# Two chunks per transpose, and edge key blocks of attention over 128 queries, in a hybrid attention and RWKV-7 block

## The chip, the cores and the metric

The kernel runs on one core of a Trainium2 chip. A core has five engines with a queue each: PE (TensorE, the matmul array, whose weight loads are listed apart as PEld), DVE (VectorE), ACT (ScalarE), POOL (GpSimd) and SP (SyncE, which here only issues transfers). The metric is the time of one execution on the device in microseconds (us), lower is better. Kernels are compared by the median of their runs.

## The reference

One layer over 2048 tokens of width 1024, in float32. Attention and a recurrence run side by side on the same normalised input, are gated and merged, and a feed-forward part follows.

```python
h = rms_norm(x, pre_mix_g); proj = h @ w_in          # q/k/v, rwkv columns, gates
# attention: 8 heads of 64; a chunk of 64 queries sees its own chunk and the 8 before it
scores = q . k * 64**-0.5 + bias[clipped distance]
y_a = softmax(scores) @ v
# RWKV-7: 8 heads of 64, state 64 x 64 per head, scan over time
state = state * w_t + (state @ a_t) b_t + v_t k_t    # a_t = -kk, b_t = kk * a
y = state @ r_t
y_b = (group_norm(y) * ln_x_w + ln_x_b + bonus) * g
merged = sigmoid(gA) * (y_a @ proj_a) + sigmoid(gB) * (y_b @ proj_b)
x = x + rms_norm(merged @ w_out, post_mix_g)
x = x + rms_norm(relu(rms_norm(x) @ w_up)**2 @ w_down, post_ffn_g)
```

## The kernel before

The tokens are worked in four groups of 512 (g = 0 to 3). For each group come a recurrence phase (phase_rwkv), attention (phase_attention) and the merge; after the four groups the feed-forward part (phase_up, phase_down) runs for all tokens. A large product is done with split operands: a float32 matrix is cut into a high and a low part, and three matmuls of 512 columns (hi by hi, hi by lo, lo by hi) replace one exact product. Those of the input projection are called psd (line 75). Each needs a block of weights, loaded by SP (wraw) and split by ACT (whi) and DVE (wlo).

The order of each engine's queue is not the order of the code: a scheduler sorts the instructions engine by engine, by its own estimates, so that psd matmuls fill the gaps of the recurrence and of attention. Any change to a step can move others.

**Recurrence.** Heads are worked in pairs p (the two heads, par = 0 and 1, on partitions 0 to 63 and 64 to 127), in chunks of 64 tokens (8 chunks, c). rwkv_pre forms the scaled operands: AR holds for each chunk three blocks of 64 columns, of which, before, slots 0 and 1 hold the decayed -kk of head 0 and of head 1 on their own rows and products of the chunk (ps_A, masked) on the other rows, and slot 2 the decayed r. rwkv_inverse inverts a unit triangular matrix per chunk by 31 steps on DVE (T and X), for two pairs of heads at a time, so twice in a group; it ends with two transposes on DVE (X, then XD), and PE's ps_t matmuls need the first. rwkv_trans then transposes A on PE (ps_at), ACT copies it into WA, and ps_w, ps_ug, ps_tq and ps_s build the transition of each chunk. recurrence runs the chunks (ps_st). rwkv_post normalises the outputs (yn), transposes them on PE (ps_yt), and ACT writes them with gain and bias into yf.

**Attention.** att_pair works a pair of heads. A half-head is 256 queries of one head, as two query blocks of 128 (b = 0, 1). A query block sees five key blocks of 128. Scores (ps_s) are reduced and exponentiated (sc), transposed on PE (ps_pt), and split by ACT into PTh and by DVE into PTl, both [128, 6 key blocks, 256 queries]. The product with the values (ps_pv, line 855) runs over six key blocks, PTh and then PTl, all 256 queries wide. Key block 0 belongs to query block 0 alone and key block 5 to query block 1 alone; the other 128 columns of these two hold zeros, set once per group (lines 906 and 907).

Of the kernel before, what the change touches and what calls it, by code (L numbers as in the profile page):

```python
# [17 lines left out]
P = 128  # L18
# [7 lines left out]
C = 64  # L26
NC = G // C
# [22 lines left out]
class Block:  # L50
# [75 lines left out]
    def constants(self, ctx, mixing):  # L126
        tc, nc, a = self.tc, self.nc, self.a
        keep = ctx.enter_context(tc.tile_pool(name="const", bufs=1))
        cp = mixing.enter_context(tc.tile_pool(name="mconst", bufs=1, side="right"))
# [38 lines left out]
        for t in self.st:  # L168
# [5 lines left out]
        rows = [("gate_bias", 16), ("shift_mu", 14), ("w0", 4), ("a0", 4), ("k_k", 4),  # L174
                ("k_a", 4), ("r_k", 4), ("ln_x_w", 4), ("ln_x_b", 4)]
# [5 lines left out]
        with tc.tile_pool(name="setup", bufs=1, side="right") as sp, \  # L181
# [18 lines left out]
            ps = pp.tile([P, nrow], F32, name="ps_rows")  # L200
# [43 lines left out]
        self.rk = view("r_k", 4)  # L244
        self.gw = view("ln_x_w", 4)
        self.gb = view("ln_x_b", 4)
        self.gwo = cp.tile([C, 4], F32, name="gwo")
        self.gbo = cp.tile([C, 4], F32, name="gbo")
        nc.vector.tensor_copy(self.gwo, self.gw[C:P])
        nc.vector.tensor_copy(self.gbo, self.gb[C:P])  # L250


        self.kc = [dp.tile([P, 2, G], F32, name=f"kc{p}") for p in range(NP)]
# [90 lines left out]
    def rwkv_pre(self, g, p, rp, NA, between=lambda: None):  # L344
        nc = self.nc
        pc = slice(p * P, (p + 1) * P)
        col = slice(p, p + 1)
# [5 lines left out]
        ps = self.lora(0, p)  # L353
# [50 lines left out]
            )  # L404
        between()

        AR = rp.tile([P, NC, 3, C], F32, tag="AR", name="AR")
        BK = self.tp.tile([P, NC, 2, C], F32, tag="BK", bufs=1, name="BK")
        k3 = k.rearrange("p (c t) -> p c t", t=C)
        r3 = r.rearrange("p (c t) -> p c t", t=C)  # L410
        for par in range(2):
            rw = slice(par * C, par * C + C)
            nc.vector.scalar_tensor_tensor(
                AR[rw, :, par], k3[rw], self.nkk[rw, col], E[rw, :, 0:C], op0=ALU.mult, op1=ALU.mult
            )
        nc.vector.tensor_tensor(AR[:, :, 2], r3, E[:, :, 1 : C + 1], ALU.mult)
        tk = self.tmp("tk")
        nc.scalar.activation(tk, ta, AF.Identity, scale=self.hka[:, col], bias=self.c1[:, col])
        nc.vector.tensor_tensor(tk, tk, k, ALU.mult)
# [50 lines left out]
        for h in range(2):  # L470
            cs = slice(h * 4, h * 4 + 4)

            both = [self.pa.tile([P, 4, P], F32, tag="a", name="ps_A") for _ in range(2)]
            for j in range(4):
                c = h * 4 + j
                for par, psA in enumerate(both):
                    rw = slice(par * C, par * C + C)
                    nc.tensor.matmul(
                        psA[:, j].rearrange("p (s t) -> p s t", t=C),
                        BK[rw, c].rearrange("p s t -> p (s t)"),  # L480
                        AR[rw, c, par : 3 : 2 - par], start=True, stop=True,
                    )
            for par, psA in enumerate(both):
                ow = slice(C - par * C, P - par * C)
                for lo, w in ((0, C), (32, 32)):
                    hw = slice(par * C + lo, par * C + lo + 32)
                    nc.vector.tensor_tensor(
                        NA[hw, q, cs, 0:w],
                        psA[hw, :, lo : lo + w],
                        n2[hw, cs, par, None].to_broadcast((32, 4, w)),  # L490
                        ALU.mult,
                    )
                nc.vector.tensor_tensor(AR[ow, cs, par], psA[ow, :, 0:C], mS[ow], ALU.mult)
                nc.vector.tensor_tensor(BR[:, cs, par, 1], psA[:, :, C:P], mN[:, par, cs], ALU.mult)
        R["AR"], R["BR"] = AR, BR
        return R
# [57 lines left out]
    def rwkv_trans(self, p, R):  # L554

        nc, xp = self.nc, self.xp
        AR, SV, XT, BR = (R[x] for x in ("AR", "SV", "XT", "BR"))
        rows = [slice(0, C), slice(C, P)]
        halves = [slice(0, 4), slice(4, 8)]

        WA = xp.tile([P, NC, 2, C], F32, tag="WA", bufs=1, name="WA")
        for h, cs in enumerate(halves):
            ps = self.pa.tile([P, 4, P], F32, tag="a", name="ps_at")
            for j in range(4):
                nc.tensor.transpose(ps[:, j], AR[:, h * 4 + j, 0:2].rearrange("p s t -> p (s t)"), self.ident)
            for par in range(2):
                nc.scalar.copy(WA[rows[par], cs, 0], ps[rows[par], :, par * C : par * C + C])
        ps = self.pa.tile([P, NC, C], F32, tag="a", name="ps_w")
        for c in range(NC):
            for par in range(2):  # L570
                ow = rows[1 - par]
                nc.tensor.matmul(ps[rows[par], c], AR[ow, c, par], SV[ow, c, par], start=True, stop=True)
        nc.scalar.copy(WA[:, :, 1], ps)
        yield

        GT = xp.tile([P, NC, C], F32, tag="GT", bufs=1, name="GT")
        for h, cs in enumerate(halves):
            ps = self.pa.tile([P, 4, 2, C], F32, tag="a", name="ps_ug")
            for j in range(4):
                c = h * 4 + j  # L580
                for par in range(2):
                    nc.tensor.matmul(ps[rows[par], j], XT[rows[par], c], WA[rows[par], c], start=True, stop=True)
            nc.scalar.copy(GT[:, cs], ps[:, :, 0])
            for par in range(2):
                nc.scalar.copy(SV[rows[par], cs, par], ps[rows[par], :, 1])
        yield
        TQ = xp.tile([P, NC, 2, C], F32, tag="TQ", name="TQ")
        for h, cs in enumerate(halves):
            ps = self.pa.tile([P, 4, 2, C], F32, tag="a", name="ps_tq")
            for j in range(4):  # L590
                c = h * 4 + j
                for par in range(2):
                    nc.tensor.matmul(
                        ps[rows[par], j], GT[rows[par], c], BR[rows[par], c, par], start=True, stop=True
                    )
            nc.vector.tensor_tensor(
                TQ[:, cs, 0], ps[:, :, 0], self.id64[:, None, :].to_broadcast((P, 4, C)), ALU.add
            )
            nc.vector.tensor_tensor(TQ[:, cs, 1], ps[:, :, 1], AR[:, cs, 2], ALU.add)
        yield  # L600
        S0 = xp.tile([P, NC, C], F32, tag="S0", name="S0")
        ps = self.pa.tile([P, NC, C], F32, tag="a", name="ps_s0")
        Y = R["Y"] = self.py.tile([P, NC, C], F32, tag="y", name="ps_y")
        for c in range(NC):
            for par in range(2):
                nc.tensor.matmul(ps[rows[par], c], BR[:, c, par, 0], SV[:, c, par], start=True, stop=True)
        nc.vector.tensor_tensor(S0, ps, R["gC"][:, :, None].to_broadcast((P, NC, C)), ALU.mult)
        for c in range(NC):
            for par in range(2):
                nc.tensor.matmul(Y[rows[par], c], BR[:, c, par, 1], SV[:, c, par], start=c == 0, stop=False)  # L610
        R["TQ"], R["S0"] = TQ, S0
        R["ST"] = xp.tile([P, NC - 1, C], F32, tag="ST", name="ST")
# [16 lines left out]
    def rwkv_post(self, p, R):  # L629
# [13 lines left out]
        yield  # L643
        yf = self.tmp("yf")
        yf3 = yf.rearrange("p (c t) -> p c t", t=C)
        for h in range(2):
            ps = self.pr.tile([C, 4, P], F32, tag="wus", name="ps_yt")
            for j in range(4):
                nc.tensor.transpose(ps[:, j], yn[:, h * 4 + j], self.ident)
            cs = slice(h * 4, h * 4 + 4)  # L650
            nc.scalar.activation(
                yf3[0:C, cs], ps[:, :, 0:C], AF.Identity, scale=self.gw[0:C, col], bias=self.gb[0:C, col]
            )
            nc.scalar.activation(
                yf3[C:P, cs], ps[:, :, C:P], AF.Identity, scale=self.gwo[:, col], bias=self.gbo[:, col]
            )
# [104 lines left out]
    def att_pair(self, g, p):  # L761
# [44 lines left out]
        for par in range(2):  # L806
            bias = self.load_bias(2 * p + par)
            Kv = KK[:, par].rearrange("p h n -> p (h n)")
            for half in range(2):
# [38 lines left out]
                    nc.vector.tensor_tensor(lv, pst[:, 0:nk], hv.bitcast(F32), ALU.subtract)  # L848
                pv = self.pv.tile([P, 2 * P], F32, tag="pv", name="ps_pv")
                kts = [kt for kt in range(6) if not first or half * 2 + kt >= GT]  # L850
                terms = [(x, kt) for x in (PTh, PTl) for kt in kts]
                for i, (x, kt) in enumerate(terms):
                    kb = half * 2 + kt
                    st = VV[:, kb // GT, kb % GT, par].rearrange("p s d -> p (s d)")
                    nc.tensor.matmul(pv, st, x[:, kt], start=i == 0, stop=i == len(terms) - 1)
# [33 lines left out]
    def phase_attention(self, g):  # L889
# [5 lines left out]
        with ExitStack() as ctx:  # L895
# [6 lines left out]
            self.pts, self.npt = [], 0  # L902
            for i in range(2):
                t = [pp.tile([P, 6, 2 * P], F32R, name=f"PT{x}{i}") for x in "hl"]
                for y in t:
                    nc.gpsimd.memset(y[:, 0, P : 2 * P].bitcast(F32), 0.0)
                    nc.gpsimd.memset(y[:, 5, 0:P].bitcast(F32), 0.0)
                self.pts.append(t)
            for p in range(NP):
                self.att_pair(g, p)  # L910
# [389 lines left out]
```

## Time and profile before

| what | value |
|---|---|
| median of 3 runs | 3430.61 us (3426.16 to 3436.8) |
| profiled execution | 3436.05 us, span 3434.4 us |
| granted PE clock, mean | 0.988 |
| PE busy | 3297.5 us (96%), 19233 matmuls |
| DVE busy | 2412.8 us (70%) |
| ACT busy | 1414.1 us (41%) |
| POOL busy | 419.6 us (12%) |
| products of attention (ps_pv) | from 339.3 to 2000.2 us, in four groups |

The span runs from the first instruction to the last. Busy time of PE counts matmuls that overlap in the array once, and the end of a matmul is modelled. A wait is written "engine tile line <- engine tile line": who waited, and whose end released it, with the sum in us, the count and the longest. Line numbers are those of the kernel before.

### The profile page before, as it was taken

What the parts mean: (1) busy time and instruction counts of PE and PEld (TensorE: products, weight loads), DVE (VectorE), ACT (ScalarE), POOL (GpSimd) and SP (SyncE); (2) the same over time, 40 slices, a digit from 0 to 9 for tenths busy, and PEclk for the clock granted to TensorE, in tenths of its full rate; (3) what the DMA queues carried; (4) which work ended last, traced back from release to release, by engine and by line L of the source; (5) the groups of instructions that cost most, each with busy time, mean ns of one, the idle gap of its engine ahead of it and who ended that gap; (6) DMA issues with size and microseconds to landing.
All of it is one profiled execution on the core that took longest, in us unless ns stands there. A gap on an engine that the chain in (4) does not pass through costs nothing. (4 is left out here: it accounts for less than half of the span.)

```text
span 3434.4 us, 50373 instructions
## 1 busy us (share of the span) xinstructions
PE 3297.5 (96%) x19233; PEld 2674.4 (78%) x19233; DVE 2412.8 (70%) x4110; ACT 1414.1 (41%) x2319; POOL 419.6 (12%) x796
## 2 busy tenths in 40 slices
PE   7999999999989999989999989999999999999998
PEld 5777777777867777867777877888888878888886
DVE  5774856766865766865775865877887788676667
ACT  4434634436644435644445634333321243331112
POOL 2210002101022111012210000111200021100001
PEclk9999999999999999999999999999999999999999
DMA  5224353225373125373224276434845374343333
GB/s 146 84 82 130 130 191 113 63 90 191 113 270 123 59 87 181 120 264 123 72 88 143 90 267 217 132 117 148 297 152 182 95 241 135 117 144 98 98 98 110
DMA packets 397864, 481.10 MB, mean 140 GB/s; under 512 B 17516, under 2 KB 304432, under 8 KB 397624
## 3 DMA queue, kind: packets, MB, share of 16 engines
q1 hardware_dynamic: 346168, 364.63, 34.1%
q0 software_dynamic: 23040, 79.71, 6.1%
q10 hardware_dynamic: 28416, 33.56, 2.9%
q8 instruction: 151, 2.47, 0.3%
q14 instruction: 89, 0.73, 0.1%
HBM read 356.16 MB, written 124.81 MB: 140 GB/s over the span
## 5 line engine op out<-in xcount | busy, mean ns | idle before, releaser
L75 PE MATMUL ps_dn<-fop 128*128 128x512 f32 x3072 | 702.6, 390 | 4.1 <-DVE u L1178 4.1
L75 PEld LDWEIGHTS ps_dn<-fop 128*128 128x128 f32 x3072 | 576.7, 188 | 126.2 <-DVE u L1178 6.0
L75 PE MATMUL psd<-hh,whi 128*128 128x512 f32 x1344 | 542.8, 404 | 8.0 <-ACT whi L66 7.1
L75 PE MATMUL psd<-hl,whi 128*128 128x512 f32 x1344 | 541.7, 403 | 0.0
L75 PE MATMUL psd<-hh,wlo 128*128 128x512 f32 x1344 | 538.4, 401 | 0.6 <-DVE wlo L67 0.5
L66 ACT CAST whi<-wraw 128x1024 fp32r<-128x1024 f32 x232 | 243.2, 1049 | 516.9 <-PE psd L75 405.8
L1178 DVE TENSOR_TENSOR u<-u,ps_dn 128x512 f32<-128x512 f32 x480 | 323.3, 685 | 149.5 <-PE ps_dn L75 148.7
L67 DVE TENSOR_TENSOR wlo<-wraw,whi 128x1024 fp32r<-128x1024 f32 x232 | 282.9, 1220 | 199.1 <-ACT whi L66 180.9
L75 PEld LDWEIGHTS psd<-hh,whi 128*128 128x128 f32 x1344 | 256.9, 191 | 60.9 <-ACT whi L66 7.9
L75 PEld LDWEIGHTS psd<-hh,wlo 128*128 128x128 f32 x1344 | 256.5, 191 | 50.5 <-DVE wlo L67 2.0
L75 PEld LDWEIGHTS psd<-hl,whi 128*128 128x128 f32 x1344 | 256.8, 191 | 50.0
L66 ACT CAST fop<-wdraw 128x1024 fp32r<-128x1024 f32 x64 | 67.0, 1047 | 427.4 <-PE ps_dn L75 236.0
L1099 POOL DMA_DIRECT2D ad<-r x128 | 69.2, 541 | 586.3 <-DVE r L1098 570.2
L968 PE MATMUL ps_o<-whi,mh 128*128 128x512 f32 x256 | 103.4, 411 | 16.6 <-ACT whi L66 12.3
L75 PE MATMUL ps_p<-yh,whi 128*128 128x512 f32 x256 | 103.8, 405 | 14.6 <-DVE th L939 12.7
L66 ACT CAST s12h<-s 128x1024 fp32r<-128x1024 f32 x32 | 33.7, 1054 | 184.6 <-PE ps_u L75 184.6
L831 DVE CUSTOM_DVE_ANT_0 sc<-bias,ps_s 128x640 f32<-128x640 f32 (+4 forms) x128 | 93.4, 730 | 22.3 <-PE ps_pt L843 18.1
L836 ACT ACTIVATE sc<-sc,mn 128x640 f32<-128x640 f32 (+4 forms) x128 | 97.7, 764 | 19.3 <-DVE mn L831 18.5
L75 PE MATMUL ps_p<-yh,wlo 128*128 128x512 f32 x256 | 104.2, 408 | 0.1
L847 ACT CAST PTh<-ps_pt 128x640 fp32r<-128x640 f32 (+4 forms) x128 | 80.0, 625 | 58.7 <-PE ps_pt L843 57.6
L75 PE MATMUL ps_p<-yl,whi 128*128 128x512 f32 x256 | 103.5, 404 | 0.0
L1097 ACT ACTIVATE r<-r 128x512 f32<-128x512 f32 x128 | 80.7, 630 | 54.2 <-DVE r L1096 54.0
(352 smaller groups left out, 6668.2 us busy)
## 6 DMA issues: line engine op xcount, KB each, us to landing
wraw<-in_w_in_dram SPq DMA_DIRECT2D x168, 512.0 KB
wraw<-in_w_up_dram SPq DMA_DIRECT2D x80, 512.0 KB
ad<-r POOLq DMA_DIRECT2D x128, 256.0 KB, 2.4
wdraw<-in_w_down_dram SPq DMA_DIRECT2D x64, 512.0 KB
araw<-ad SPq DMA_DIRECT2D x64, 512.0 KB
gd<-gate ACTq DMA_DIRECT2D x64, 256.0 KB
th<-gd SPq DMA_DIRECT2D x32, 512.0 KB
wraw<-in_w_out_dram SPq DMA_DIRECT2D x32, 512.0 KB
```

Source lines behind the costliest of these rows:

```text
L66: self.nc.scalar.copy(hi, src)
L67: self.nc.vector.tensor_tensor(lo, src, hi.bitcast(F32), ALU.subtract)
L75: mm = nc.tensor.matmul(ps, l, r, start=n == 0, stop=n == last).ins
L831: nc.vector.tensor_tensor_reduce(sc[:, 0:n], bias[:, s0:640], pss[:, c0 : c0 + n], 1.0, 3.0e38, ALU.add, ALU.min, mn,)
L836: nc.scalar.activation(sc[:, 0:n], sc[:, 0:n], AF.Exp, scale=-1.0, bias=mn, accum_out=sm)
L847: nc.scalar.copy(hv, pst[:, 0:nk])
L968: nc.tensor.matmul(ps[t], l[:, k, ts], r[:, k % 2], start=k == 0 and j == 0, stop=k == KB - 1 and j == 2)
L1097: nc.scalar.activation(r, r, AF.Relu)
L1099: nc.gpsimd.dma_start(self.ad[fb][:, th], r)
L1178: nc.vector.tensor_tensor(u[t][:, ns], u[t][:, ns], ps, ALU.add)
```

## The change

AR is laid out anew, as three planes over all chunks: plane 0 the decayed -kk of both heads, plane 1 the decayed r, plane 2 what ps_A gives. So one DVE instruction on 128 rows writes what two on 64 rows wrote, and two chunks stand side by side for one 128x128 transpose. The transposes of A take two chunks each (4 for a pair of heads instead of 8), and so do the transposes of yn. What comes out for the odd chunks lies on the other half of the partitions, so gain and bias are kept for both halves (gwb).

In attention, key block 0 multiplies only the queries of block 0, and key block 5 only those of block 1, with 128 columns each. No zeros are needed, and the memsets go. [...]

```diff
-        self.gwo = cp.tile([C, 4], F32, name="gwo")
-        self.gbo = cp.tile([C, 4], F32, name="gbo")
-        nc.vector.tensor_copy(self.gwo, self.gw[C:P])
-        nc.vector.tensor_copy(self.gbo, self.gb[C:P])
+        self.gwb = cp.tile([P, 2, 2, 4], F32, name="gwb")
+        for i, src in enumerate((self.gw, self.gb)):
+            for par in range(2):
+                for e in range(2):
+                    nc.vector.tensor_copy(self.gwb[e * C : e * C + C, i, par], src[par * C : par * C + C])
...
-        AR = rp.tile([P, NC, 3, C], F32, tag="AR", name="AR")
+        AR = rp.tile([P, 3, NC, C], F32, tag="AR", name="AR")
...
-        for par in range(2):
-            rw = slice(par * C, par * C + C)
-            nc.vector.scalar_tensor_tensor(
-                AR[rw, :, par], k3[rw], self.nkk[rw, col], E[rw, :, 0:C], op0=ALU.mult, op1=ALU.mult
-            )
-        nc.vector.tensor_tensor(AR[:, :, 2], r3, E[:, :, 1 : C + 1], ALU.mult)
+        nc.vector.scalar_tensor_tensor(
+            AR[:, 0], k3, self.nkk[:, col], E[:, :, 0:C], op0=ALU.mult, op1=ALU.mult
+        )
+        nc.vector.tensor_tensor(AR[:, 1], r3, E[:, :, 1 : C + 1], ALU.mult)
...
-        for h, cs in enumerate(halves):
-            ps = self.pa.tile([P, 4, P], F32, tag="a", name="ps_at")
-            for j in range(4):
-                nc.tensor.transpose(ps[:, j], AR[:, h * 4 + j, 0:2].rearrange("p s t -> p (s t)"), self.ident)
-            for par in range(2):
-                nc.scalar.copy(WA[rows[par], cs, 0], ps[rows[par], :, par * C : par * C + C])
+        ps = self.pa.tile([P, NC // 2, P], F32, tag="a", name="ps_at")
+        for j in range(NC // 2):
+            nc.tensor.transpose(ps[:, j], AR[:, 0, 2 * j : 2 * j + 2].rearrange("p c t -> p (c t)"), self.ident)
+        for par in range(2):
+            for e in range(2):
+                nc.scalar.copy(WA[rows[par], e:NC:2, 0], ps[rows[e], :, par * C : par * C + C])
...
-        for h in range(2):
-            ps = self.pr.tile([C, 4, P], F32, tag="wus", name="ps_yt")
-            for j in range(4):
-                nc.tensor.transpose(ps[:, j], yn[:, h * 4 + j], self.ident)
...
+        ps = self.pr.tile([P, NC // 2, P], F32, tag="wus", name="ps_yt")
+        for j in range(NC // 2):
+            nc.tensor.transpose(ps[:, j], yn[:, 2 * j : 2 * j + 2].rearrange("p c t -> p (c t)"), self.ident)
+        for par in range(2):
+            for e in range(2):
+                rw, er = slice(par * C, par * C + C), slice(e * C, e * C + C)
+                scale, bias = (self.gwb[er, i, par, col] for i in range(2))
+                nc.scalar.activation(
+                    yf3[rw, e:NC:2], ps[er, :, par * C : par * C + C], AF.Identity, scale=scale, bias=bias
+                )
...
-                terms = [(x, kt) for x in (PTh, PTl) for kt in kts]
+                edge = {0: slice(0, P), 5: slice(P, 2 * P)}
+                full = [kt for kt in kts if kt not in edge]
+                terms = [(PTh, kt) for kt in full]
+                terms += [(x, kt) for x in (PTh, PTl) for kt in kts if kt in edge]
+                terms += [(PTl, kt) for kt in full]
...
-                    nc.tensor.matmul(pv, st, x[:, kt], start=i == 0, stop=i == len(terms) - 1)
+                    qs = edge.get(kt, slice(0, 2 * P))
+                    nc.tensor.matmul(pv[:, qs], st, x[:, kt, qs], start=i == 0, stop=i == len(terms) - 1)
...
-                for y in t:
-                    nc.gpsimd.memset(y[:, 0, P : 2 * P].bitcast(F32), 0.0)
-                    nc.gpsimd.memset(y[:, 5, 0:P].bitcast(F32), 0.0)
```

The scheduler makes a new order of the four groups from it; the feed-forward part keeps its own. Three places follow. The first is DVE's queue at the end of the first inverse of group 1, before: T and X are the last steps, wlo is the low half of a block of weights, v a mixed input of the next pair of heads, and X<-X and XD<-X are the two transposes.

```order
L511 TENSOR_TENSOR T<-N,X 128x30
L517 TENSOR_TENSOR X<-X,T 128x2x15
L511 TENSOR_TENSOR T<-N,X 128x16
L67 TENSOR_TENSOR wlo<-wraw,whi 128x1024
L517 TENSOR_TENSOR X<-X,T 128x16
L301 SCALAR_TENSOR_TENSOR v<-pr,cst,v 128x512
L520 STREAM_TRANSPOSE X_5864<-X 128x32x16
L522 STREAM_TRANSPOSE XD<-X_5864 128x512
```

The same place now:

```order
L511 TENSOR_TENSOR T<-N,X 128x30
L517 TENSOR_TENSOR X<-X,T 128x2x15
L511 TENSOR_TENSOR T<-N,X 128x16
L517 TENSOR_TENSOR X<-X,T 128x16
L520 STREAM_TRANSPOSE X_5815<-X 128x32x16
L67 TENSOR_TENSOR wlo<-wraw,whi 128x1024
L522 STREAM_TRANSPOSE XD<-X_5815 128x512
L303 SCALAR_TENSOR_TENSOR v<-pr,cst,v 128x512
```

The weight split and the mix of v have moved behind the transpose that PE waits for. On PE, 9 psd fewer stand ahead of the ps_t of each group's first inverse (from the last ps_a on, 31 instead of 40), and 10 psd more between it and the ps_t of the second, where 8 ps_at and 8 ps_yt have gone.

The second place is PE's queue right behind that, before: ps_t<-XT,Z ends the inverse, ps_at are the transposes of A, ps_w follows when ACT has copied.

```order
L548 MATMUL ps_t_6070<-XT,Z 32x32 x31
L565 MATMUL ps_at<-ident,AR 128x128 x4
L75 MATMUL psd<-hh,whi 128x512
L75 MATMUL psd<-hl,whi 128x512
L75 MATMUL psd<-hh,wlo 128x512
L75 MATMUL psd<-hh,whi 128x512
L75 MATMUL psd<-hl,whi 128x512
L565 MATMUL ps_at<-ident,AR 128x128 x4
L75 MATMUL psd<-hh,wlo 128x512
L572 MATMUL ps_w<-SV,AR 64x64 x16
```

The same place now:

```order
L548 MATMUL ps_t_6021<-XT,Z 32x32
L564 MATMUL ps_at<-ident,AR 128x128 x4
L548 MATMUL ps_t_6021<-XT,Z 32x32 x31
L75 MATMUL psd<-hh,whi 128x512
L75 MATMUL psd<-hl,whi 128x512
L75 MATMUL psd<-hh,wlo 128x512
L75 MATMUL psd<-hh,whi 128x512
L75 MATMUL psd<-hl,whi 128x512
L75 MATMUL psd<-hh,wlo 128x512
L572 MATMUL ps_w<-SV,AR 64x64 x16
```

One run of four transposes is gone, and six psd still stand between the transposes and ps_w.

The third place is PE's queue at the first half-head of attention in group 1, before, from the second query block's transposes of the probabilities (ps_pt) on; ps_s are scores of later query blocks.

```order
L843 MATMUL ps_pt<-ident,sc 128x128 x5
L75 MATMUL psd<-hh,whi 128x512
L75 MATMUL psd<-hl,whi 128x512
L75 MATMUL psd<-hh,wlo 128x512
L75 MATMUL psd<-hh,whi 128x512
L75 MATMUL psd<-hl,whi 128x512
L825 MATMUL ps_s<-KK,QA 128x320
L855 MATMUL ps_pv<-PTh_7790,VV 128x256 x5
L855 MATMUL ps_pv<-PTl_7791,VV 128x256
L825 MATMUL ps_s<-KK,QB 128x320
L825 MATMUL ps_s<-KK,QA 128x320
L825 MATMUL ps_s<-KK,QB 128x320
```

The same place now, from the last psd ahead of the scores on:

```order
L75 MATMUL psd<-hh,whi 128x512
L75 MATMUL psd<-hl,whi 128x512
L75 MATMUL psd<-hh,wlo 128x512
L825 MATMUL ps_s<-KK,QA 128x320
L861 MATMUL ps_pv<-PTh_7699,VV 128x256 x4
L861 MATMUL ps_pv<-PTh_7699,VV 128x128 x2
L861 MATMUL ps_pv<-PTl_7700,VV 128x128 x2
L861 MATMUL ps_pv<-PTl_7700,VV 128x256 x4
L843 MATMUL ps_pt<-ident,sc 128x128 x5
L825 MATMUL ps_s<-KK,QB 128x320
L825 MATMUL ps_s<-KK,QA 128x320
L825 MATMUL ps_s<-KK,QB 128x320
```

Before, the first key block's product went ahead of all this, and the last five with PTl came later, behind three score matmuls. Now all twelve stand together, with seven psd (three are shown) instead of five between the transposes and the scores.

More of the change, by code (lines that the diff above doesn't have):

```diff
@@ L480, in rwkv_pre @@
                         BK[rw, c].rearrange("p s t -> p (s t)"),
-                        AR[rw, c, par : 3 : 2 - par], start=True, stop=True,
+                        AR[rw, 0:2, c], start=True, stop=True,
                     )
@@ L492, in rwkv_pre @@
                     )
-                nc.vector.tensor_tensor(AR[ow, cs, par], psA[ow, :, 0:C], mS[ow], ALU.mult)
+                nc.vector.tensor_tensor(AR[ow, 2, cs], psA[ow, :, 0:C], mS[ow], ALU.mult)
                 nc.vector.tensor_tensor(BR[:, cs, par, 1], psA[:, :, C:P], mN[:, par, cs], ALU.mult)
@@ L571, in rwkv_trans @@
                 ow = rows[1 - par]
-                nc.tensor.matmul(ps[rows[par], c], AR[ow, c, par], SV[ow, c, par], start=True, stop=True)
+                nc.tensor.matmul(ps[rows[par], c], AR[ow, 2, c], SV[ow, c, par], start=True, stop=True)
         nc.scalar.copy(WA[:, :, 1], ps)
@@ L598, in rwkv_trans @@
             )
-            nc.vector.tensor_tensor(TQ[:, cs, 1], ps[:, :, 1], AR[:, cs, 2], ALU.add)
+            nc.vector.tensor_tensor(TQ[:, cs, 1], ps[:, :, 1], AR[:, 1, cs], ALU.add)
         yield
@@ L645, in rwkv_post @@
         yf3 = yf.rearrange("p (c t) -> p c t", t=C)
-        for h in range(2):
-            ps = self.pr.tile([C, 4, P], F32, tag="wus", name="ps_yt")
-            for j in range(4):
[L649 to L656, printed above, removed]
+        ps = self.pr.tile([P, NC // 2, P], F32, tag="wus", name="ps_yt")
[8 more added lines that the diff above has]
+                )
         bv = self.tmp("bv")
```

## The prediction

> **What bounds the kernel now.** The page first: its span, its busy times, and TensorE's row of the 40 slices.
>
> ```profile
> span 3434.4 us, 50373 instructions
> PE 3297.5 (96%) x19233; PEld 2674.4 (78%) x19233; DVE 2412.8 (70%) x4110; ACT 1414.1 (41%) x2319; POOL 419.6 (12%) x796
> PE   7999999999989999989999989999999999999998
> ```
>
> PE, the matmul array, is busy for 96% of the span. So the time is what PE has to issue plus the few places where it stands. The question for each edit is whether it takes issue time from PE, or shortens one of those stands. Where they lie in one recurrence phase (token group 1) the view of busy time by stretch shows: the stretch, then PE, weight loads, VectorE (DVE), ScalarE (ACT), GpSimd (POOL), the granted clock, and DMA.
>
> ```profile
> core 0: us, PE busy (x) PEld busy (x) DVE busy (x) ACT busy (x) POOL busy (x), PEclk, DMA share, GB/s
> 620.00:630.00 10.00, 8.00 (x36) 6.29 (x34) 9.46 (x28) 5.85 (x10) 1.53 (x6) 1.00 0.18 52
> 640.00:650.00 10.00, 10.00 (x167) 8.44 (x167) 1.88 (x6) 3.76 (x11) 0.75 (x4) 1.00 0.20 56
> 650.00:660.00 10.00, 9.76 (x144) 7.76 (x141) 2.14 (x4) 5.53 (x15) 3.67 (x5) 1.00 0.08 28
> 720.00:730.00 10.00, 9.42 (x47) 7.44 (x45) 9.28 (x29) 6.89 (x12) 0.64 (x1) 1.00 0.58 186
> 790.00:800.00 10.00, 10.00 (x50) 8.25 (x49) 5.26 (x8) 5.90 (x11) 2.40 (x10) 1.00 0.62 211
> 840.00:850.00 10.00, 10.00 (x58) 8.28 (x57) 7.79 (x16) 6.76 (x14) 0.96 (x3) 1.00 0.53 179
> ```
>
> PE is full at 640 to 660, where the transposes of A stand, at 790 to 800, where the second transposes of the outputs stand, and at 840 to 850, inside attention. At 620 to 630 it is not: there DVE is full (9.46 of 10) with the serial inverse. The list of waits names that place, and the stretches of 2 us around one such wait show what follows it.
>
> ```profile
> PE ps_t L541 <- DVE X L520: 26.7, 8, 3.8
> 628.00:630.00 2.00, 0.00 (x1) 0.00 (x0) 2.00 (x4) 0.14 (x1) 0.05 (x1) 1.00 0.00 0
> 630.00:632.00 2.00, 1.15 (x59) 1.16 (x60) 1.97 (x3) 1.04 (x2) 0.13 (x1) 0.87 0.81 237
> 632.00:634.00 2.00, 2.00 (x18) 1.65 (x14) 1.99 (x5) 1.96 (x4) 0.00 (x0) 0.50 0.12 34
> 634.00:636.00 2.00, 2.00 (x8) 1.58 (x8) 1.99 (x3) 1.54 (x4) 0.00 (x0) 0.77 0.00 0
> ```
>
> At the end of all eight inverses (two in each of four groups) PE stands until DVE has transposed X, 26.7 us in total, 3.3 us each. After it the granted clock falls to 0.50, then 0.77.
>
> **Part 1, the transposes.** The first two rows are groups of instructions (form, count, total busy, mean ns of one); the next are from the order in time (start, length).
>
> ```profile
> L565 PE MATMUL ps_at<-ident,AR 128*128 128x128 f32 x128 | 20.9, 287 | 0.0
> L649 PE MATMUL ps_yt<-ident,yn 128*64 128x128 f32 x128 | 17.8, 272 | 0.0
> 640.06 0.60 PE L565 MATMUL ps_at<-ident,AR 128*128 128x128 f32 x4
> 719.28 1.03 PE L649 MATMUL ps_yt<-ident,yn 128*64 128x128 f32 x8
> ```
>
> One alone takes 0.27 us, but a run of them overlaps: eight ps_yt in 1.03 us are (1.03 - 0.27) / 7 = 0.11 us each, four ps_at in 0.60 us are (0.60 - 0.27) / 3 = 0.11 each. So PE pays 0.11 for each. Full-width operands (128*128, what ps_yt becomes) cost the same 0.11 as the narrower 128*64, so the new ps_yt is no dearer. Each kind falls from 128 to 64: 2 x 64 x 0.11 = **-14 us of PE**. ACT copies the same numbers of elements in as many instructions (four of 64x256 per pair of heads, both times), so it costs and gains nothing. Those copies now start after one run of four transposes, as the first of them did before, so the chain to ps_w is not longer.
>
> **Part 2, the edge blocks.** They are 4 of 12 products per pair of query blocks in groups 1 to 3 (48 such pairs) and 2 in group 0 (16 pairs): 224, each now over 128 columns where it was 256. The trace has 256 columns for these products, and 128 columns of the same data type in group 0's scores.
>
> ```profile
> 838.14 0.75 PE L855 MATMUL ps_pv<-PTl,VV 128*128 128x256 f32 x5
> 329.30 0.39 PE L75 MATMUL psd<-hl,whi 128*128 128x512 f32 x1
> 329.53 0.39 PE L75 MATMUL psd<-hh,wlo 128*128 128x512 f32 x1
> 329.75 0.22 PE L825 MATMUL ps_s<-KK,QA 128*128 128x128 f32 x1
> 329.81 0.28 PE L825 MATMUL ps_s<-KK,QB 128*128 128x128 f32 x1
> 329.92 0.45 PE L75 MATMUL psd<-hh,whi 128*128 128x512 f32 x1
> 330.21 0.39 PE L75 MATMUL psd<-hl,whi 128*128 128x512 f32 x1
> 647.55 1.05 PE L386 MATMUL ps_ss<-bones,sq 128*128 128x2 f32 x8
> ```
>
> Five products of 256 columns in 0.75 us are (0.75 - 0.28) / 4 = 0.118 each. A 512-column matmul holds PE for 0.23 (329.30 to 329.53). From 329.53 to 330.21 there are two of those and the two of 128 columns: (0.68 - 0.46) / 2 = 0.11 for one of 128. Even a matmul of 2 columns is not cheaper: eight ps_ss in 1.05 us, 0.11 to 0.13 each. So below 256 columns there is a floor, and an edge saves 0.118 - 0.11 = 0.008 us: 224 x 0.008 = **-2 us**, not half of the cost. The bounds are 0 (the floor is higher) and half the pitch, 224 x 0.059 = -13; I stay at -2, since two rows of 128 and 2 columns both stand at the floor.
>
> [...]
>
> **Part 3, VectorE and the end of the inverse.** Two half-height writes of A become one.
>
> ```profile
> L413 DVE SCALAR_TENSOR_TENSOR AR<-k,nkk,E 64x512 f32<-64x512 f32 x32 | 23.9, 746 | 3.5 <-ACT E L372 2.8
> L301 DVE SCALAR_TENSOR_TENSOR k<-pr,cst,k 128x512 f32<-128x512 f32 x16 | 12.0, 748 | 0.0
> 624.43 0.75 DVE L413 SCALAR_TENSOR_TENSOR AR<-k,nkk,E 64x512 f32<-64x512 f32 x1
> 627.85 1.23 DVE L67 TENSOR_TENSOR wlo<-wraw,whi 128x1024 fp32r<-128x1024 f32 x1
> 628.99 0.17 DVE L517 TENSOR_TENSOR X<-X,T 128x16 f32<-128x16 f32 x1
> 629.07 0.75 DVE L301 SCALAR_TENSOR_TENSOR v<-pr,cst,v 128x512 f32<-128x512 f32 x1
> 629.74 1.06 DVE L520 STREAM_TRANSPOSE X<-X 128x512 f32<-128x512 f32 x1
> ```
>
> A 128-row instruction of this kind lasts as long as a 64-row one (748 against 746 ns), so 16 x 0.75 = 12 us leave DVE. One of them stands inside the first inverse of each group (624.43). There the new order also moves the weight split wlo and the mix of v from ahead of the transpose of X to behind it: 628.99 - 627.85 = 1.14 and 629.74 - 629.07 = 0.67. ps_t is released 0.75 + 1.14 + 0.67 = 2.6 us earlier. But PE gets there earlier too, with 9 psd fewer ahead of it, 9 x 0.23 = 2.1. So the stand shrinks by 0.5 us in each first inverse, and those 9 psd follow later, where PE is full. Between the first and the second inverse PE loses 8 ps_at and 8 ps_yt (1.8 us, already counted) and gets 10 psd (2.3): it comes 0.5 us later there, while DVE has one instruction of 0.75 less, and starts that much sooner if it is the chain. I take 0.9 us. Four groups: 4 x (0.5 + 0.9) = **-5.5 us** of standing. Bounds: 0, if DVE's lead is eaten by its own waits for PE, and 4 x (2.6 + 0.75) = -13, all of DVE's lead.
>
> **Part 4, the products' waits in attention.** Before, the block kt = 0 could go as soon as the first query block's PTh was there; now all of them follow the second PTh, and after six products PE needs the second PTl.
>
> ```profile
> PEld ps_pv L855 <- ACT PTh L847: 31.1, 92, 0.6
> PEld ps_pv L855 <- DVE PTl L848: 3.3, 15, 0.3
> 829.08 0.82 DVE L848 TENSOR_TENSOR PTl<-ps_pt,PTh 128x640 fp32r<-128x640 f32 x1
> ```
>
> The 48 early products had waits of 31.1 / 92 = 0.34 us at the weight load (not all of it PE's, which still had a psd to finish): their going is worth 0 to 48 x 0.34 = -16 us. PTl lasts 0.82 us from the end of PTh, and the products ahead of it last 4 x 0.118 + 3 x 0.11 = 0.80, so a DVE that is free makes PE wait next to nothing. One that is late by half an instruction makes it wait 0.4 us, 64 x 0.4 = +26. Both ends look alike from here; I take 0.
>
> **Part 5, the rest.** The memsets of PTh and PTl (32) leave POOL, which is 12% busy: nothing. Six more constant copies stand on DVE at the start.
>
> ```profile
> L249 DVE COPY gwo<-cst 64x4 f32<-64x4 f32 x1 | 0.2, 164 | 0.0
> ```
>
> That is 6 x 0.164 = 1.0 us, beside the first weight loads: 0 to +1, I take +0.5. Nothing changes behind the mixing part; the up and down projections keep their order.
>
> **Sum:** -14 - 2 - 5.5 + 0 + 0.5 = -21 us. The profiled execution took 3436 us with a span of 3434.4, so it would be 3415. It lies 5.4 us above the median of the three runs shown (3430.6), so the forecast on that scale is 3410, 0.6% faster. About 0.3%, 10 us, is what a measurement of this kernel can tell from no change.
>
> **Rivals.**
> *The wait for PTl (slower).* PE's queue now goes from PTh to PTl without a psd between them. Behind a late PTl stand the scores and transposes of the next query block, on which ACT and DVE wait in turn. With w us at each of the 64 half-heads the change is lost at w = 21 / 64 = 0.33, and slower by 0.3% from w = 31 / 64 = 0.49. For it: DVE is busy for 7.8 of 10 us in the attention row above, and an instruction of 0.7 to 0.8 us can stand ahead of PTl. Against it: only 15 such waits now, 0.22 each, and the new order puts 7 psd and a score, not 5, between the transposes of the probabilities and the products. At w = 0.6: 38 - 21 = +17, so 3448. Chance 0.09.
> *Only the full stretches pay.* If what PE saves before each inverse's end turns into standing there, what counts is the transposes after the second inverse (half of 14) and the edges: -9, so 3422. For it: DVE at 9.28 to 9.46 of 10 in the inverses; against it: the order brings DVE's end forward as well. Chance 0.17.
> *The edges at half price.* Then -13 and not -2: 3399. The row of 2 columns speaks against it. [...] Chance 0.06.
> *The clock stays up.* After each stand PE runs about 2 us at 0.50, 2 at 0.77 and 2 at 0.87: 1.0 + 0.46 + 0.26 = 1.7 us lost, 14 us in eight. If shorter stands no longer bring the clock down, it is 3396. Against it: about 2.3 to 3 us remain of each. [...] Chance 0.10.
>
> **How the numbers follow.** The sum as it stands has 0.58, with a range of its own from 3402 to 3419. With the edges and the clock rivals, faster by over 0.3% (below 3420) has 0.74. The full-stretches rival is within 0.3%: 0.17. The wait for PTl is slower: 0.09. The range goes from 3398 to 3427: it leaves out the slower rival, half of the clock's, and little of the others.
>
> **What the profile after would show.** Right: 64 ps_at and 64 ps_yt at a pitch of 0.11; edge products at 0.11; PE's wait for X around 21 us, not 26.7; waits of the weight load for PTl below 10 us in total; the page's span near 3413. Wrong: 128-column products at 0.06 (the floor is not there), a wait for X that has grown by what the transposes gave, or PTl at the head of PE's waits in attention.

## The result and the profile after

The changed kernel takes 3436.59 us (median of 20 runs, 3428.7 to 3445.27), the kernel before 3428.86 (20 runs, 3424.74 to 3437.94). The ratio is 1.002, 95% interval 1.0012 to 1.0027: 7.7 us slower, where 21 us less were forecast. First the page of the changed kernel:

```profile
span 3438.7 us, 49994 instructions
PE 3291.8 (96%) x19105; PEld 2668.0 (78%) x19105; DVE 2400.7 (70%) x4100; ACT 1416.3 (41%) x2319; POOL 406.2 (12%) x764
```

The groups of the two kinds of transposes (shortest, median and longest duration in ns, first and last start), and then a run of one kind in the order in time:

```profile
L564 PE MATMUL ps_at<-ident,AR x64: 272/273/474, 154.2 to 1807.7; 128*128 128x128 f32 x64
L649 PE MATMUL ps_yt<-ident,yn x64: 270/272/273, 238.6 to 1845.3; 128*128 128x128 f32 x64
```

```profile
789.14 0.60 PE L649 MATMUL ps_yt<-ident,yn 128*128 128x128 f32 x4
```

The transposes are halved and cost what was said: (0.60 - 0.27) / 3 = 0.11 us each, also at full width. PE is busy 5.7 us less, and yet the span grows by 4.3. So PE stands longer. These are the waits of PE and of its weight loads (PEld) after (sum, count, longest).

```profile
PE ps_t L541 <- DVE X L520: 25.1, 8, 3.8
PE pstr L120 <- DVE xn L290: 17.1, 5, 10.1
PE ps_s L825 <- ACT KK L770: 11.1, 3, 4.1
PE psd L75 <- DVE QA L783: 3.7, 1, 3.7
PEld ps_pt L843 <- DVE PTl L848: 11.8, 23, 0.8
PEld ps_pv L861 <- DVE PTl L848: 10.6, 29, 0.7
```

And those of before that answer to them:

```profile
PE pstr L120 <- DVE xn L288: 10.4, 2, 10.3
PE psd L75 <- DVE QA L783: 0.8, 1, 0.8
PE ps_s L825 <- ACT KK L770: 0.6, 3, 0.2
PEld ps_pt L843 <- DVE PTl L848: 1.3, 4, 0.4
```

The wait for X at the inverse's end went from 26.7 to 25.1 only. New are 11.1 and 3.7 us at the start of attention (ps_s for KK in groups 1 to 3, psd for QA in group 0), and waits for PTl inside it (ps_pv had 3.3 us of them, as the prediction shows). The longer wait of pstr for xn stands at the end of the merge in groups 1 and 2 (3.1 and 3.2 us), where before ps_o waited 4.3 and 4.4 us for a weight cast; in the four merges together PE is idle for 40.3 us, before for 38.5. Set against the starts of the same instructions before, the stages of the four groups together changed by:

| stage (from, to) | after minus before, us |
|---|---|
| recurrence (to the last ps_g) | -14.0 |
| start of attention (last ps_g to first ps_s) | +12.4 |
| attention (first ps_s to last ps_pv) | +1.0 |
| merge (to the last ps_o) | +7.4 |
| feed-forward | -2.1 |

What the recurrence gains, the first microseconds of attention lose. The row of attention is too good and that of the merge too bad: 28 products of the merge (ps_p, 0.23 us each, 6.4 us) that were worked before the last ps_pv now come behind it, so attention itself lost some 7 us and the merge 1. And 32 of the 128 transposes saved lie behind the last ps_g, 3.5 us of gain within the start of attention. The order in time shows what that start lost; ScalarE at the start of attention in group 1, before (in brackets the idle time ahead and what ended it):

```profile
796.33 1.06 ACT L66 CAST whi<-wraw 128x1024 fp32r<-128x1024 f32 x1 [2.49 <-PE psd L75]
797.29 0.58 ACT L780 ACTIVATE QA<-psd 64x512 fp32r<-64x512 f32 x1
799.96 0.60 ACT L780 ACTIVATE QA<-psd 64x512 fp32r<-64x512 f32 x1 [1.49 <-DVE QA L783]
801.07 1.03 ACT L770 CAST KK<-kr 128x1024 fp32r<-128x1024 f32 x1
802.61 1.05 ACT L66 CAST whi<-wraw 128x1024 fp32r<-128x1024 f32 x1
```

and after, with the first scores of PE:

```profile
796.86 1.05 ACT L66 CAST whi<-wraw 128x1024 fp32r<-128x1024 f32 x1 [1.64 <-PE psd L75]
797.94 0.59 ACT L780 ACTIVATE QA<-psd 64x512 fp32r<-64x512 f32 x1
802.30 1.04 ACT L66 CAST whi<-wraw 128x1024 fp32r<-128x1024 f32 x1 [3.17 <-PE psd L75]
803.37 0.59 ACT L780 ACTIVATE QA<-psd 64x512 fp32r<-64x512 f32 x1
804.96 1.04 ACT L770 CAST KK<-kr 128x1024 fp32r<-128x1024 f32 x1 [0.39 <-DMA kr<-kc]
806.05 0.64 PE L825 MATMUL ps_s<-KK,QA 128*128 128x320 f32 x1 [3.57 <-ACT KK L770]
```

SyncE's queue at the same place, which issues the loads of kr (the keys of the group before, from which the cast KK is made) and of wraw; before:

```profile
791.20 0.42 SPq L769 DMA_DIRECT2D kr<-kc  x1
800.75 0.38 SPq L60 DMA_DIRECT2D wraw<-in_w_in_dram  x1
```

and after:

```profile
799.20 0.37 SPq L60 DMA_DIRECT2D wraw<-in_w_in_dram  x1
799.62 0.68 SPq L769 DMA_DIRECT2D kr<-kc  x1
```

The stretches of 2 us from there (columns as in the prediction; the granted clock stands behind POOL's):

```profile
804.00:806.00 2.00, 0.00 (x0) 0.00 (x0) 1.96 (x3) 1.61 (x2) 0.00 (x0) 0.81 1.02 391
806.00:808.00 2.00, 1.95 (x5) 1.70 (x6) 0.75 (x3) 1.20 (x4) 0.59 (x4) 0.50 1.16 339
808.00:810.00 2.00, 2.00 (x6) 1.58 (x5) 1.35 (x2) 0.58 (x1) 0.70 (x1) 0.50 0.79 273
810.00:812.00 2.00, 2.00 (x6) 1.52 (x6) 0.00 (x0) 1.04 (x1) 0.00 (x0) 0.50 0.87 316
812.00:814.00 2.00, 2.00 (x10) 1.65 (x9) 0.10 (x1) 0.62 (x1) 0.00 (x0) 0.99 0.80 267
```

The cast whi, which cuts the next block of weights, now stands ahead of the second QA. It waits 3.17 us for PE to finish with the old block, and QA, QB and KK stand behind it in ACT's queue. In SP's queue the load of kr has slid behind a load of weights too, which waited until DVE had split an earlier block (to 799.17): kr is issued at 799.62 instead of 791.20. KK waits for both, and the load came last: ACT was free 0.39 us before kr had landed, 0.92 and 0.28 us in groups 2 and 3. So the cast alone, put back, would not have brought KK forward while the load stayed late; in group 0, which has no kr, QA waits behind the split of the weights only, and PE stands for 3.7 us all the same. PE stands for 3.57 us, and then runs at a granted clock of 0.50 for some 6 us. The clock also fell to 0.50 at the stands of 2.5 us at the inverses' ends of the changed kernel (the first of each group, 2.51 to 2.53 us).

### The profile page after: what moved, and what is told of

Read it like the earlier page. It is cut to its first block, busy times and chain, and to the rows that moved or that the text cites. A ratio compares the mean times of both kernels' runs of the same rounds, so it can differ in the third digit from the quotient of the medians.

```text
span 3438.7 us, 49994 instructions
## 1 busy us (share of the span) xinstructions
PE 3291.8 (96%) x19105; PEld 2668.0 (78%) x19105; DVE 2400.7 (70%) x4100; ACT 1416.3 (41%) x2319; POOL 406.2 (12%) x764
## 5 line engine op out<-in xcount | busy, mean ns | idle before, releaser
L75 PE MATMUL ps_p<-yh,whi 128*128 128x512 f32 x256 | 104.7, 409 | 14.7 <-DVE th L942 11.4
L848 DVE TENSOR_TENSOR PTl<-ps_pt,PTh 128x640 fp32r<-128x640 f32 (+4 forms) x128 | 94.4, 737 | 20.1 <-ACT PTh L847 19.0
L971 PE MATMUL ps_o<-wlo,mh 128*128 128x512 f32 x256 | 102.4, 400 | 3.8 <-DVE wlo L67 3.8
```

The source lines that it names most:

```text
L75: mm = nc.tensor.matmul(ps, l, r, start=n == 0, stop=n == last).ins
L971: nc.tensor.matmul(ps[t], l[:, k, ts], r[:, k % 2], start=k == 0 and j == 0, stop=k == KB - 1 and j == 2)
```

## The experiments

Each is compared with the kernel before, run on the same chip beside it; differences below are of medians.

| run | us, and before | ratio, 95% interval |
|---|---|---|
| rec_only | 3435.28, 3433.08 | 1.0006, 0.9996 to 1.0016 |
| edges_only | 3445.92, 3433.08 | 1.0040, 1.0027 to 1.0053 |
| rec_fixed | 3421.22, 3433.08 | 0.9965, 0.9953 to 0.9977 |
| after_fixed | 3432.04, 3433.08 | 0.9994, 0.9984 to 1.0003 |
| order_only | 3427.73, 3433.61 | 0.9981, 0.9972 to 0.9989 |
| width_only | 3451.60, 3433.61 | 1.0048, 1.0033 to 1.0063 |
| best_of_both | 3434.18, 3433.61 | 1.0003, 0.9994 to 1.0013 |
| narrow_wide_order | 3425.22, 3430.67 | 0.9982, 0.9973 to 0.9992 |
| wide_narrow_order | 3440.82, 3430.67 | 1.0027, 1.0016 to 1.0037 |
| rec_fixed_order | 3407.49, 3430.67 | 0.9934, 0.9918 to 0.9950 |
| rec_fixed_order_narrow | 3409.90, 3430.67 | 0.9939, 0.9927 to 0.9951 |
| after_other_queues | 3415.98, 3429.26 | 0.9962, 0.9949 to 0.9976 |
| no_cover | 3432.24, 3430.58 | 1.0005, 0.9996 to 1.0015 |

### Which part moves the cast

**rec_only** takes the edits of the recurrence and leaves attention, with its memsets, as before.

> Only the edits of the recurrence (three planes of AR, transposes of two chunks); attention as before. Displaced casts (my theory): the new order of ACT's queue at the start of attention, a weight cast ahead of the second QA and QB, comes with these edits alone. Then PE saves the 14 us that the recurrence phases gained in the changed kernel's trace and loses 12 us in the four starts of attention: 2 us faster than before, within 5 us of it, with PE waits of ps_s for KK over 8 us. Edges to blame (rival): the loss belongs to the edits of attention; then this one is 12 to 16 us faster and ps_s waits for KK 0.6 us as before.

**edges_only** takes the edits of attention and leaves the recurrence as before.

> Only the edits of attention (edge products of 128 columns, full key blocks first, no memsets); the recurrence as before. Displaced casts: the starts of attention stay as before (ps_s waits for KK under 1 us), and steady attention moved by only 1 us in the changed kernel's trace, so the difference to before is between -3 and +5 us. Edges to blame: 18 to 22 us slower, since these edits then carry the 8 us of loss and the 14 that the recurrence gained.

**rec_fixed** and **after_fixed** hold the cast back. For the first pair of heads of a group the next block of weights, its load and its split, is queued behind the load of kr and the first KK from psd (in short):

```diff
+            ca = nc.scalar.copy(KK[rw, par, 1], ps[rw])
+            cd = nc.vector.tensor_tensor(KK[ow, par, 1], ps[rw], ...)
...
+        # wraw, whi and wlo of the next block:
+        with tc.issue_after(ca.ins), tc.issue_after(cd.ins), tc.issue_after(dk.ins):   # dk: the load of kr
```

> The edits of the recurrence alone, and for the first pair of heads of each group the next block of weights is loaded and split behind the first KK cast from psd (issue order only, on SP, ACT and DVE). Displaced casts: the 12 us of the four starts of attention come back, so 10 to 16 us faster than before. Rival (the place of the cast is harmless, PE only stands where it would have stood later): the same as with the edits of the recurrence alone, within 3 us.

> The whole change, and the next block of weights of the first pair of heads loaded and split behind the first KK cast from psd. Displaced casts: 12 us come back of the changed kernel's loss of 8, so 1 to 8 us faster than before. Rival (the place of the cast is harmless): 5 to 10 us slower than before, like the changed kernel.

Measured: the recurrence alone +2.2 us, with the block held back -11.9, both as the theory of displaced casts had them. PE's wait for KK in rec_only, and what is left of it in rec_fixed:

```profile
PE ps_s L825 <- ACT KK L770: 12.6, 3, 4.7
```

```profile
PE ps_s L839 <- ACT KK L778: 0.9, 3, 0.3
```

So the edits of the recurrence, not those of attention, put the block of weights there, and its place costs 2.2 + 11.9 = 14.1 us: as much as the transposes were to give. The scheduler draws other places anew too when the block is held, so the 14.1 is not the block's alone: in the traces the start of attention differs by 16.1 us between the two runs (+12.8 and -3.3 against before), and the other stages take 4.1 of it back. Nor is it the cast's alone. The edit holds back the load as well as the split, and in rec_only, too, kr landed last, 0.3 to 1.5 us after ACT was free. How much each of the two costs by itself was not tried. In the whole change holding the block gave 8.7 us (from +7.7 to -1.0). But edges_only, expected between -3 and +5, came out at +12.8: attention loses by itself, and the stage table had hidden that, since the merge's products had moved out of its row.

### Order, width or queues

My theory was then that PE stands for PTl because the new order reaches it sooner, and the rival that narrow products cost more than they seem. **order_only** has the new order of the twelve products, all at 256 columns. **width_only** has narrow edges in nearly the old order (key block 0 with the first PTh, as before). **best_of_both** is rec_fixed with width_only.

```diff
-                    qs = edge.get(kt, slice(0, 2 * P))      # changed kernel
+                    qs = slice(0, 2 * P)                    # order_only, zeros kept
...
-                terms = [(PTh, kt) for kt in full] + ...
+                terms = [(PTh, kt) for kt in (kts if first else [0, 5, 1, 2, 3, 4])]   # width_only
+                terms += [(PTl, kt) for kt in kts]
```

> The kernel before, with only the new order of the twelve products (full key blocks with PTh, the four edges, full ones with PTl); all are 256 columns wide and the zeros stay. Late PTl (my theory): PE reaches PTl six products after the second PTh and stands there and at the next transposes, and the early product with key block 0 is gone; 8 to 14 us slower than before, weight loads of ps_pv and ps_pt waiting over 15 us for PTl in sum. Narrow products (rival): what costs is the width of 128 and the slow products after it; then this one is within 3 us of before.

> The kernel before, with edge products of 128 columns and no zeros, in nearly the old order: key block 0 first, as soon as the first PTh is there, then 5, then the full ones, then PTl in the old order. Late PTl: the waits stay as before and the edges give their 2 us, so between 5 us faster and 2 us slower than before, the weight loads of ps_pv waiting under 6 us for PTl. Narrow products: 8 to 14 us slower.

> The edits of the recurrence, the weight cast held behind KK at the start of attention, and edges of 128 columns in nearly the old order. Late PTl: the 12 us of the recurrence with the cast held back, and 0 to 3 more from the edges: 10 to 17 us faster than before. Narrow products: 2 us slower to 5 us faster than before, as the whole change with the cast held back.

All three went against the theory: -5.9, +18.0 and +0.6. The rival has only the last within its range, and the products themselves are not slower. (The full key blocks need not go first, as width_only also shows: in groups 1 to 3 its first two products of a sum are the narrow ones of key blocks 0 and 5, with 128 columns each, and the sums come out right.) Two half-heads in the order in time, order_only first (256 columns), then narrow_wide_order (below):

```profile
835.79 0.97 PE L861 MATMUL ps_pv<-PTh,VV 128*128 128x256 f32 x6
836.61 0.28 PE L861 MATMUL ps_pv<-PTl,VV 128*128 128x256 f32 x1
838.12 0.76 PE L861 MATMUL ps_pv<-PTl,VV 128*128 128x256 f32 x5
```

```profile
838.86 0.91 PE L861 MATMUL ps_pv<-PTh,VV 128*128 128x256 f32 x6
839.60 0.28 PE L861 MATMUL ps_pv<-PTl,VV 128*128 128x128 f32 x1
841.14 0.74 PE L861 MATMUL ps_pv<-PTl,VV 128*128 128x128 f32 x5
```

Six PTh products take 836.61 - 835.79 = 0.82 us wide and 839.60 - 838.86 = 0.74 with two narrow ones: a little less, not more. That left the queues that the scheduler draws. In width_only, for one, PE's waits of the merge for a weight cast grew from 2.0 (before, second fence) to 13.1; what else makes up its 18.0 us was not taken apart:

```profile
PE ps_p L75 <- ACT whi L66: 13.1, 2, 9.0
```

```profile
PE ps_p L75 <- ACT whi L66: 2.0, 1, 2.0
```

The second theory, queue order, was tested by building the program twice: the order of every engine's queue is taken from the one width and forced on the other.

```diff
+    order = build(narrow=False)          # the queues that the scheduler makes for 256 columns
+    nc = build(narrow=True, order=order) # the same queues, edges of 128
...
+        for a, b in zip(names, names[1:]):      # for each engine
+            tc.add_manual_dep(traced[b], a, NoSync)
```

> Twelve products as with the new order alone, but the edges 128 columns wide, while every engine's queue is held to exactly the order that the scheduler makes for edges of 256 columns. Queue order (my second theory: the narrow products are as cheap as they look, but the scheduler draws other queues for them, and those cost): 5 to 12 us faster than before, 0 to 5 us faster than the new order alone. Narrow products (rival: the width itself costs on PE): 6 to 16 us slower than before.

> The mirror of it: edges of 256 columns with the zeros kept, every queue held to exactly the order that the scheduler makes for edges of 128 columns, that of the run with the edits of attention alone. Queue order: 8 to 16 us slower than before, as with the edits of attention alone. Narrow products: 3 to 9 us faster than before, as with the new order of the products alone.

This settles it: narrow edges in the wide queues -5.4 us, wide edges in the narrow queues +10.2. The width changes the time by 0.4 us (-5.45 against -5.88) in the wide queues and by 2.7 (12.84 of edges_only against 10.15) in the narrow ones, with overlapping intervals; at 256 columns the queues change it by 16.0 (10.15 + 5.88). In the traces the stretches between the first ps_s and the last ps_pv of the groups differ by 2.3, 3.8, 3.2 and 3.7 us, as much as the spans (13.1); what the other stages gain and lose cancels. The waits of the weight loads show a part of it. order_only, then wide_narrow_order:

```profile
PEld ps_pv L861 <- DVE PTl L848: 2.0, 10, 0.3
PEld ps_pt L843 <- DVE PTl L848: 1.5, 5, 0.4
```

```profile
PEld ps_pv L861 <- DVE PTl L848: 9.8, 29, 0.7
PEld ps_pt L843 <- DVE PTl L848: 9.5, 21, 0.8
```

### What in the queues

With 256 columns the scheduler mostly puts scores or psd between the first product with PTl and the other five; with 128 columns it mostly puts nothing. By the traces the two stand together in 16 of the 64 half-heads before and in 19 in order_only, but in 49 in the changed kernel and in 52 in edges_only. **no_cover** is narrow_wide_order with this one thing moved, on PE's queue alone (one half-head):

```diff
 MATMUL ps_pv<-PTh 128x256 x4
 MATMUL ps_pv<-PTh 128x128 x2
-MATMUL ps_pv<-PTl 128x128
+MATMUL ps_pv<-PTl 128x128 x2
+MATMUL ps_pv<-PTl 128x256 x4
 MATMUL ps_s<-KK,QA 128x320
 MATMUL ps_s<-KK,QB 128x320
-MATMUL ps_pv<-PTl 128x128
-MATMUL ps_pv<-PTl 128x256 x4
 MATMUL ps_pt<-ident,sc 128x128 x5
```

> Edges of 128 columns in the queues that the scheduler makes for 256 (5.4 us faster than before), with one thing moved on PE's queue alone: the last five products with PTl stand right behind the first in every half-head, as in the changed kernel, and the scores or psd that stood between follow them. Missing cover (theory): PE stands for PTl, the weight loads of ps_pv wait over 8 us for it in sum, and 8 to 15 us of time are lost, so 3 to 10 us slower than before. Rival (the loss lies elsewhere in the queues): within 3 us of the kernel with the cover, so 2 to 8 us faster than before.

```profile
827.41 0.91 PE L863 MATMUL ps_pv<-PTh,VV 128*128 128x256 f32 x6
828.16 0.28 PE L863 MATMUL ps_pv<-PTl,VV 128*128 128x128 f32 x1
829.05 0.85 PE L863 MATMUL ps_pv<-PTl,VV 128*128 128x128 f32 x5 [0.62 <-DVE PTl L849]
```

narrow_wide_order, with the cover, and then no_cover:

```profile
PEld ps_pv L861 <- DVE PTl L848: 3.8, 13, 0.5
PEld ps_pv L863 <- DVE PTl L849: 11.4, 31, 0.8
```

no_cover loses 7.1 us against narrow_wide_order (+1.7 against -5.4), and PE's weight loads wait 11.4 us for PTl where they waited 3.8 (13 times) with the cover. Expected were 8 to 15, or by the rival under 3; so the missing cover is shown to cost about 7 of the 16 us. The rest is open: ps_pt waits 9.5 us for PTl in wide_narrow_order and 1.3 in no_cover, so the other moves in the queues are the likely place, but none was tried alone.

### Putting it together

**rec_fixed_order** is rec_fixed with order_only; **rec_fixed_order_narrow** the same queues with narrow edges; **after_other_queues** has all edits of the change (the memsets stay), no cast held back, and the queues drawn for wide edges.

> The edits of the recurrence, the weight cast held behind KK, and the new order of the twelve products at 256 columns with the zeros. If the gains add up (12 and 6 us): 14 to 22 us faster than before. If they are one gain in the queues that only shows once: 8 to 13 us.

> The same, with edges of 128 columns, every queue held to the order that the scheduler makes for 256. Queue order: 0 to 5 us faster than with 256 columns, so 14 to 26 us faster than before. Narrow products: 10 to 18 us slower than with 256 columns, so within 6 us of before.

> All edits of the changed kernel but one (the zeros are still set), with every queue held to the order that the scheduler makes when the edges are 256 columns; the weight cast is not held behind KK. Sum of parts: the recurrence's edits alone gave +2, the new order of the products -6, the narrow edges in a held queue -2, so 6 us faster than before (2 to 11), where the changed kernel is 7 us slower; the weight loads of ps_pv wait under 6 us for PTl, and ps_s still waits over 8 us for KK. Rival (the parts don't add up, the slower queues of one stage cover those of another): within 2 us of before, or slower.

Measured: -23.2, -20.8 and -13.3. The gains add up (11.9 and 5.9 make 17.8; it was 5 more, with 17.8 still inside the interval). The best kernel, rec_fixed_order, beats before by 0.66%, still with all edges at 256 columns; with narrow edges it is 2.4 us slower, not up to 5 faster, within the intervals. after_other_queues gained 7 us more than the 6 expected, which stays unexplained; the block of weights ahead of KK still costs, and most of its PTl waits are gone:

```profile
PE ps_s L825 <- ACT KK L770: 12.2, 3, 4.8
PEld ps_pv L861 <- DVE PTl L848: 2.9, 13, 0.3
```

Nearly the same instructions as in the changed kernel thus take 3416 us in one order and 3437 in another.

## Why the prediction was wrong

**Part 1, the transposes (-14).** The count and the pitch of 0.11 were right. Of the 14.0 us that the recurrence phases gained in the trace, the 96 transposes saved there are 10.6. With the start of attention set right, the edits of the recurrence gave 11.9.

**Part 2, the edges (-2).** Next to nothing, as said: in held queues the narrow edges changed the time by +0.4 us, and by +2.7 and +2.4 in two other pairs. Half price, the rival, is excluded: it would be -13. The sign of 0.06, which was to speak for it, came all the same, but for one pair only: in the changed kernel's trace the two narrow products with PTh start 0.06 us apart and the product behind them 0.11 later, while the two with PTl start 0.17 apart (medians of the 48 half-heads with six key blocks).

**Part 3, the stand for X (-5.5).** Too large: 26.7 became 25.1, so 1.6. At the first inverses it came nearly as counted: in group 1, counted from the start of the phase, DVE is done 2.4 us earlier and PE arrives 2.1 earlier, and the stand shrinks by 0.3 (0.5 forecast). From there to the second inverse the two shift by the same amount (in group 1 both take 1.2 us longer), so the 0.9 there became 0.1: DVE's lead of 0.75 did not show, as at the lower bound. The clock's rival is excluded too: at all eight of these stands, now 2.5 to 3.8 us long, the clock fell to 0.50.

**Part 4, the products' waits (0).** This is the first step that failed. Two things are in it. The new order with wide edges, in which the early product is gone, was worth 5.9 us together with its queues (order_only), between my bounds of 0 and 16. PTl was costed as if what stands around the products stayed as it was before; I even counted the psd ahead of them, and not what stood between the first product with PTl and the other five. That cover went away with the narrow edges: 7.1 us for it alone, 16.0 for all the queues that come with them. The rival "the wait for PTl" had the mechanism, with a price of 38 us and a chance of 0.09; at the weight loads of ps_pv and ps_pt the waits came to 10.6 and 11.8 us, from 3.3 and 1.3 before, where the prediction wanted them below 10 in all; PE itself stood for PTl for 3.6 and 3.0 us.

**Part 5, the rest (+0.5).** This is the second step that failed: "nothing changes behind the mixing part" was about the projections, and the first instructions of attention were not looked at at all. There the edits of the recurrence moved a block of weights ahead, its load ahead of kr's and its cast ahead of the second QA: 14.1 us, with what else the scheduler moves. The memsets, removed or kept, change no other queue: the orders of the remaining instructions are the same.

So, in medians: -11.9 (recurrence) + 14.1 (block of weights) - 5.9 (order) + 16.0 (queues of narrow edges) + 0.4 (width) = +12.7, where +7.7 was measured; with the width's 2.7 of the narrow queues it is +15.0. The signs and the two large terms are shown; 5 to 7 us of overlap between parts is not resolved. One place for it, not shown to be the cause: the changed kernel's attention begins at a granted clock of 0.50 in groups 1 to 3 (for 6.8 us each, from 805.2, 1330.9 and 1859.9 us on), and PE then stands 8.7 us in the four stages, where in edges_only it stands 17.0.

## What to carry to other kernels

Where a scheduler orders the queues, an edit costs what it does to the queues too: look in the new order, at every stage that follows the edit, for an instruction with a long wait that has moved ahead of work that PE needs, and for independent work that has left the gap between a product and its late operand. Before an edit is judged, run it in the old queues and the old work in the new queues. Look at the loads as well: of the two things that KK waited for, the load landed last. A gain of 12 us was here hidden by one block of weights whose load and cast had slid ahead, and it came back by holding that block behind the work that PE waits for.

## What the runs showed of the hardware

Two narrow products save more issue time than the floor of 0.11 allowed, (0.82 - 0.74) / 2 = 0.04 us each among the six with PTh shown above (0.03 at the half-head before, 829.11 - 828.29 = 0.82 in order_only against 832.12 - 831.36 = 0.76 in narrow_wide_order); the five with PTl save next to nothing (0.76 against 0.74 us, with one of the five narrow). And still the kernel is not faster by it.

The granted clock came back late: after the stand of 3.57 us it stayed at 0.50 from 806 to 812 us with PE full. How long it stayed down did not follow from the length of the stand. In the two traces every stretch at 0.50 but the last lasts 3.4 or 6.8 us. In the kernel before, two stands of 2.8 us at the end of an inverse were followed by 3.4 us of it (631.5 to 634.9) and by 6.8 (1682.8 to 1689.6), and a third, which ended at 1154.7, by none.
